# A pooled-mixer layer: a hand-written step order replaced by a planned instruction order, two products accumulated in PSUM, and the last two products done row by row

## The chip, the cores and the metric

One core of one Trainium2 chip runs the whole program. The metric is the device time of one execution in microseconds (us); lower is better. The kernel before was timed three times.

## The reference, cut to what matters

With the given depth of 1 only the pooled mixer runs, and then a layer norm over the sum of the scaled input and the mixer's output. All data is float32; the sequence has 2048 positions, the model width is 1024.

```python
h = x @ w_in                                   # 1024 -> 2 * 2048
u, z = h[..., :D_POOL], h[..., D_POOL:]
...
for g, w in enumerate((2, 4, 8, 16)):          # four groups of 512 channels
    outs.append((c - lag) / cnt - u[:, :, g])  # mean of the last w positions, minus u
m = einsum('bsgc,gcd->bsgd', stack(outs), w_grp).reshape(B, S, D_POOL) * scale
y = (m * silu(z)) @ w_out                      # 2048 -> 1024
out = layer_norm(DN_ALPHA * x + y, ln_g, ln_b)
```

## The kernel before, in words

**Stages.** The group matrix commutes with the pooling over positions, so the kernel first multiplies the u half of `w_in` by `w_grp` (`fold`, 16 steps, four per group) and stores the product in DRAM (`wv_d`). Then it takes the sequence in two halves `h` of 1024 positions. For each half it makes, for eight column pairs `p` in the order 4, 5, 6, 7, 2, 3, 0, 1, one block of z and one block of the values v (`up`, kinds z and v, 256 columns each), pools v along positions, gates it with silu(z) and the scale, and stores the result in DRAM (`g_d`). Then `down` multiplies the stored blocks by `w_out`, adds the scaled input and does the layer norm. So the stages are: fold, ups of half 0, down of half 0, ups of half 1, down of half 1.

**Arithmetic.** Every product is done to nearly float32 accuracy: each operand is split into a high part (a copy to the 32-bit replicated format on ScalarE, line 116) and a low remainder (a subtraction on VectorE, line 117), and one product is three matmuls: high times high, high times low, low times high (`mm3`, lines 122 to 124). A block product of 2 by 2 blocks is done with seven block products and not eight (Strassen-Winograd). The sums of blocks that this needs are VectorE work: of the left and right operands before (lines 129 to 134, 280 to 290, 582 to 588), and of the results after. `fold` has 8 `mm3` in a step; one `up` has 7 products of 4; one `down` has 7 products over 8 values of `k` and 4 row blocks `m`. All matmuls are 128 by 128 by 512.

**Results in `up`.** Seven products go to three PSUM banks Y, Z, W. The first product is copied from Y to SBUF, the second (Z) is added there, and further products are accumulated onto Y and W in PSUM; ScalarE copies from the banks (line 328) and VectorE adds (line 331). Where a combination is missing it is made by adding two SBUF blocks (line 331 with `dest(0, 1)` as operand). A z block passes through silu (lines 328 and 355). A v block is then pooled by repeated shifted additions (line 373), scaled and reduced by v (line 383), gated (line 391), and its block sums are made; three DMAs store it (lines 414 to 416). At the end of a `down`, `read` adds bank and residual into row tiles (lines 492, 494) and takes statistics (496); `norm` (503 to 512) makes the layer norm of a block of 128 rows, with a power on GpSimd for the reciprocal root (505), and stores it (515, 517).

**What sets the order.** The work is a list of `steps`, each of which is the matmuls of one step and the reads of their banks. Loads and splits are `Job`s with `Part`s, taken strictly in one written order. Pooling, sums and norms are `Task`s in a queue with a written due step. After the matmuls of each step, the loop at the end of the file spends a budget (`BUDGET`, in arbitrary units) on the next parts and the most urgent tasks. A load is issued when its place in a ring is free: `raw` tiles hold loaded operands (three places of 8 KB per partition, shared by loads of the fold, x, z, v, `w_out` and the residual), `w2` tiles hold split operands (five places), z tiles two, the v tile one, and the n tiles for the pooling two. Every DMA goes through SyncE's queue (SPq). What is written here is a program order; the framework beneath it assigns semaphores and may itself move an instruction on a queue.

**Last product.** In the down of half 1 the last of the seven products runs row by row: all its operands are split beforehand into tiles freed by x (`spare`), and each of the four row blocks is finished, read and normalised before the next.

Of the kernel before, what the change touches and what calls it, by code (L numbers as in the profile page):

```python
# [12 lines left out]
P = 128  # L13
# [3 lines left out]
NG = 4  # L17
# [10 lines left out]
MT = HS // P  # L28
B = 512
OFF = 16  # L30
# [3 lines left out]

W2 = 5
RAW = 3
BUDGET = 4.2
# [7 lines left out]
A_SLOT = (0, 1, 4, 3, 5, 6, 2)  # L45


class Task:


    def __init__(self, ready, due, cost, run):
        self.ready, self.due, self.cost, self.run = ready, due, cost, run
# [3 lines left out]
def pool_mixer_kernel(ctx: ExitStack, tc, x, xT, wuT, wz, wg, scale, wo, ln_g, ln_b, out):  # L56
# [9 lines left out]
    nc = tc.nc  # L66

# [18 lines left out]
    wv_d = [dr.tile([P, 2, KD // 2, 2 * P], F32, name=f"wv{p}") for p in range(NP)]  # L86
    g_d = [[dr.tile([P, 7, B], F32, name=f"g{h}_{p}") for p in range(NP)] for h in range(2)]
    wt_d = [dr.tile([P, 4, B], F32, name=f"wt{k}") for k in range(NP)]

# [3 lines left out]
    def psum():  # L93
        return ps.tile([P, B], F32, name="acc")

    stores = []
    taken = {"raw": 0, "w2": 0}
    places = {"raw": RAW, "w2": W2}

    def take(kind):  # L100

        for t in [t for t in stores if t[2] is not None and t[2][0] == kind and t[2][1] <= taken[kind] - places[kind]]:
            stores.remove(t)
            t[1]()
        taken[kind] += 1

    def raw_tile():
        take("raw")
        return rp.tile([P, 4, B], F32, name="raw")

    def w2_tile():
        take("w2")
        return wp.tile([P, 2, 2, B], F32R, name="w2")

    def split(hi, lo, src):
        nc.scalar.activation(hi, src, AF.Copy)  # L116
        nc.vector.tensor_sub(lo, src, f32(hi))  # L117

    def mm3(o, a, b, first, last):

        (ah, al), (bh, bl) = a, b
        nc.tensor.matmul(o, ah, bh, start=first, stop=False, skip_group_check=True)  # L122
        nc.tensor.matmul(o, ah, bl, start=False, stop=False, skip_group_check=True)  # L123
        nc.tensor.matmul(o, al, bh, start=False, stop=last, skip_group_check=True)  # L124

    def sums(t, a11, a21, a12, a22):

        def one():
            nc.vector.scalar_tensor_tensor(t[:, 0], a21, -1.0, a22, op0=OP.mult, op1=OP.subtract)
            nc.vector.scalar_tensor_tensor(t[:, 1], t[:, 0], -1.0, a11, op0=OP.mult, op1=OP.subtract)  # L130

        def two():
            nc.vector.tensor_sub(t[:, 2], a11, a21)
            nc.vector.tensor_sub(t[:, 3], a12, t[:, 1])
        return one, two


    steps = []
    jobs = []
    queue = []  # L140
    now = [-1]
    written = set()

    def step(run, reads=()):
        steps.append((run, list(reads)))
        return len(steps) - 1

    class Part:


        def __init__(self, first, last, cost, run, w2=True, ready=-1):
            self.first, self.last, self.cost, self.run, self.w2, self.ready = first, last, cost, run, w2, ready

    class Job:


        def __init__(self, raws, load, parts, until=None, needs=()):
            self.raws, self.load, self.parts, self.until, self.needs = raws, load, parts, until, needs
            self.left, self.loaded = len(parts), False

        def done(self):
            return self.left == 0 and (self.until is None or now[0] >= self.until)

    def store(f, late=2, place=None):

        stores.append((now[0] + late, f, place))

    def later(ready, due, cost, run):
        queue.append(Task(ready, due, cost, run))


    accs = {}

    def fold(g, c):
        me, w = {}, {}

        def load():
            r = g * GC + c * P
            me["raw"] = raw = raw_tile()
            nc.sync.dma_start(raw[:, 2], wg[g, c * P:(c + 1) * P, :])  # L180
            for b in range(2):
                nc.sync.dma_start(raw[:, b], wuT[r:r + P, b * B:(b + 1) * B])

        def part0():
            w["g"] = t = w2_tile()
            split(t[:, 0, 0], t[:, 1, 0], me["raw"][:, 2])

        def part1():
            w["u"] = t = w2_tile()
            for b in range(2):  # L190
                split(t[:, 0, b], t[:, 1, b], me["raw"][:, b])

        def run():
            if c == 0:
                accs[g] = [psum() for _ in range(KD)]
            for m in range(KD):
                cols = slice((m % 4) * P, (m % 4 + 1) * P)
                mm3(accs[g][m], (w["u"][:, 0, m // 4, cols], w["u"][:, 1, m // 4, cols]),
                    (w["g"][:, 0, 0], w["g"][:, 1, 0]), c == 0, c == KC - 1)

        def evict():
            for half in range(2):
                e = zp.tile([P, 4, B], F32, name="z")
                for k in range(4):
                    if k % 2 == 0:
                        nc.scalar.activation(e[:, k], accs[g][half * 4 + k], AF.Copy)  # L206
                    else:
                        nc.vector.tensor_copy(e[:, k], accs[g][half * 4 + k])

                def out_(half=half, e=e):  # L210
                    for q in range(2):
                        nc.sync.dma_start(wv_d[2 * g + q][:, half], e[:, :, q * 2 * P:(q + 1) * 2 * P])
                        written.add(("wv", 2 * g + q, half))
                store(out_, 1)

        s = step(run, [evict] if c == KC - 1 else [])
        jobs.append(Job(1, load, [Part(s, s, 1, part0), Part(s, s, 2, part1)]))


    xh, xl = {}, {}  # L220

    def x_job(h, k, half, first, ready):
        me = {}
        Q = B // 2
        cols = slice(half * Q, (half + 1) * Q)

        def load():
            me["raw"] = raw_tile().rearrange("p a (b c) -> p (a b) c", b=2)
            for a in range(2):
                kk = k + a * KD // 2  # L230
                src = xT[kk * P:(kk + 1) * P, h * HS:(h + 1) * HS].rearrange("p (a b) -> p a b", a=2)
                nc.sync.dma_start(me["raw"][:, 2 * a:2 * a + 2], src[:, :, cols])

        def p0():
            if half == 0:
                xh[h, k] = xp.tile([P, 7, B], F32R, name="xh")
                xl[h, k] = xp.tile([P, 7, B], F32R, name="xl")
            raw = me["raw"]
            me["sums"] = sums(raw[:, 4:8], raw[:, 0], raw[:, 1], raw[:, 2], raw[:, 3])
            me["sums"][0]()  # L240

        def p1():
            me["sums"][1]()

        def part(a, b, c):
            return lambda: split(xh[h, k][:, a:a + c, cols], xl[h, k][:, a:a + c, cols], me["raw"][:, b:b + c])

# [4 lines left out]
    zs = {}  # L252

    def up(h, p, kind):
        me, w, acc = {}, {}, {}
        base = len(steps)


# [478 lines left out]
```

## Time and profile before

| | |
|---|---|
| median of 3 runs | 1066.22 us (1066.04 to 1067.38) |
| the profiled execution: time, span | 1066.48 us, 1064.7 us |
| matmuls | 4435, of them 19 to warm up |
| busy: PE, VectorE, ScalarE, GpSimd | 1023.5, 825.0, 418.6, 30.6 us |
| moved by DMA | 186.39 MB, 175 GB/s on the mean |

The span is the time from the first to the last instruction of the trace. In the trace PE is TensorE's matmuls, PEld its weight loads, DVE VectorE, ACT ScalarE, POOL GpSimd, SPq SyncE's queue of DMA issues. Line numbers are those of the kernel above. A row of the windows view gives, for a stretch of time, each engine's busy time and, in brackets, how many instructions began in it, then the clock that TensorE was granted, the share of the DMA engines' time that was used, and the rate. In a row of the timeline, "[3.12 <-ACT z L328]" says that the engine stood idle for 3.12 us before it and what released it. A busy matmul row is longer than the distance to the next one, because matmuls are pipelined.

### The profile page before, as it was taken

To read this page: it belongs to the slowest core of one execution; us is meant where nothing else is said; L and a number is where in the kernel's file an instruction comes from. 1 tells how busy PE (TensorE), PEld (TensorE's weight loads), DVE (VectorE), ACT (ScalarE), POOL (GpSimd) and SP (SyncE) were. 2 spreads that over 40 slices of the span, in tenths; PEclk is the share of its full clock that TensorE was granted. 3 is DMA by queue.
4 is the path that set the end of the run, shared out by engine and by line. 5 is a ranking of instruction groups with operands and counts; after the bars stand their busy time and mean duration, and the time that the engine had idled before them with its cause. 6 is when DMAs were issued, how large, how long until landed. Compare 5 with 4: busy or idle time off the path is not lost.

```text
span 1064.7 us, 11976 instructions
## 1 busy us (share of the span) xinstructions
PE 1023.5 (96%) x4435; PEld 833.7 (78%) x4435; DVE 825.0 (77%) x1057; ACT 418.6 (39%) x546; POOL 30.6 (3%) x45
## 2 busy tenths in 40 slices
PE   9899899999989999899999999999999999999994
PEld 7777788787868888787788787888878888888883
DVE  6777586988868975887689996968868876765678
ACT  5564433343333334254453343433333334343430
POOL 0000000000000000000002200000000000000003
PEclk9999999999999999899999999999999999999998
DMA  8887525344343355686777423312222325777743
GB/s 263 251 271 253 188 74 193 141 166 148 128 178 148 133 191 192 213 270 223 232 237 257 158 90 99 114 74 109 89 100 109 135 82 190 260 251 238 233 163 158
DMA packets 78746, 186.39 MB, mean 175 GB/s; under 512 B 7392, under 2 KB 24288, under 8 KB 71520
## 3 DMA queue, kind: packets, MB, share of 16 engines
q1 hardware_dynamic: 78688, 185.64, 50.3%
q8 instruction: 34, 0.56, 0.2%
q14 instruction: 24, 0.20, 0.1%
HBM read 131.08 MB, written 54.53 MB: 174 GB/s over the span
## 4 chain that ended last, share of the span: by engine, by line
PE 54%; DVE 23%; DMA 13%; issue 5%; ACT 3%; SPq 1%; POOL 0%; DVEq 0%; POOLq 0%; ACTq 0%
PE acc L122 18%; PE acc L124 18%; PE acc L123 18%; DVE w L117 6%; DMA raw<-in_xT 3%; DMA raw<-wt 3%; DVE n L373 3%; DMA g<-v 2%; DVE xl L117 2%; DVE z L391 1%; DVE n L383 1%; ACT w L116 1%; DMA raw<-in_wo 1%; DVE stats L496 1%; DVE z L512 1%
## 5 line engine op out<-in xcount | busy, mean ns | idle before, releaser
L117 DVE TENSOR_TENSOR w<-raw,w 128x1024 fp32r<-128x1024 f32 (+1 forms) x280 | 295.4, 1067 | 130.7 <-ACT w L116 128.6
L116 ACT ACTIVATE w<-raw 128x1024 fp32r<-128x1024 f32 (+1 forms) x280 | 258.5, 935 | 332.3 <-PE acc L124 131.5
L122 PE MATMUL acc<-xh,w 128*128 128x512 f32 x896 | 350.6, 394 | 11.2 <-ACT z L328 7.1
L124 PE MATMUL acc<-xh,w 128*128 128x512 f32 x896 | 348.2, 391 | 1.8 <-DVE w L117 1.8
L123 PE MATMUL acc<-xl,w 128*128 128x512 f32 x896 | 349.7, 390 | 0.0
L122 PEld LDWEIGHTS acc<-xh,w 128*128 128x128 f32 x896 | 168.9, 189 | 54.4 <-ACT z L328 9.6
L124 PEld LDWEIGHTS acc<-xh,w 128*128 128x128 f32 x896 | 168.7, 188 | 39.4 <-DVE w L117 3.7
L123 PEld LDWEIGHTS acc<-xl,w 128*128 128x128 f32 x896 | 169.1, 189 | 34.1
L122 PE MATMUL acc<-w 128*128 128x512 f32 x416 | 163.2, 396 | 6.1 <-ACT w L116 6.1
L123 PE MATMUL acc<-w 128*128 128x512 f32 x416 | 164.5, 395 | 1.5 <-DVE w L117 1.5
L124 PE MATMUL acc<-w 128*128 128x512 f32 x416 | 163.9, 394 | 0.0
L122 PEld LDWEIGHTS acc<-w 128*128 128x128 f32 x416 | 79.4, 191 | 24.1 <-ACT w L116 7.4
L123 PEld LDWEIGHTS acc<-w 128*128 128x128 f32 x416 | 79.6, 191 | 19.3 <-DVE w L117 2.5
L328 ACT ACTIVATE v<-acc 128x512 f32<-128x512 f32 x80 | 46.3, 597 | 118.8 <-PE acc L124 108.4
L124 PEld LDWEIGHTS acc<-w 128*128 128x128 f32 x416 | 79.5, 191 | 16.6
L328 ACT ACTIVATE z<-acc 128x512 f32<-128x512 f32 x80 | 47.3, 595 | 85.0 <-PE acc L124 69.8
L116 ACT ACTIVATE xh<-raw 128x1024 fp32r<-128x1024 f32 (+2 forms) x52 | 38.0, 730 | 53.3 <-DMA raw<-in_xT 31.6
L373 DVE TENSOR_TENSOR n<-n 128x1024 f32<-128x1024 f32 (+3 forms) x48 | 58.5, 1220 | 0.2
L122 PE MATMUL acc<-w,w 128*128 128x512 f32 x128 | 50.2, 392 | 3.6 <-ACT z L206 3.1
L124 PE MATMUL acc<-w,w 128*128 128x512 f32 x128 | 50.0, 392 | 1.7 <-DVE w L117 1.6
L123 PE MATMUL acc<-w,w 128*128 128x512 f32 x128 | 49.9, 390 | 0.0
L373 DVE TENSOR_TENSOR n<-v 128x1030 f32<-128x1030 f32 (+3 forms) x32 | 39.2, 1229 | 12.5 <-ACT v L328 12.5
(79 smaller groups left out, 695.8 us busy)
## 6 DMA issues: line engine op xcount, KB each, us to landing
raw<-g SPq DMA_DIRECT2D x112, 256.0 KB, 4.2
raw<-in_wz SPq DMA_DIRECT2D x16, 1024.0 KB, 4.8
raw<-wv SPq DMA_DIRECT2D x16, 1024.0 KB, 5.2
g<-v SPq DMA_DIRECT2D x16, 1024.0 KB, 5.0
raw<-wt SPq DMA_DIRECT2D x64, 256.0 KB, 4.5
raw<-in_wo SPq DMA_DIRECT2D x48, 256.0 KB, 4.7
raw<-in_wuT SPq DMA_DIRECT2D x32, 256.0 KB, 5.4
raw<-in_xT SPq DMA_DIRECT2D x32, 256.0 KB, 5.1
```

The lines of the kernel that those rows point to most:

```text
L116: nc.scalar.activation(hi, src, AF.Copy)
L117: nc.vector.tensor_sub(lo, src, f32(hi))
L122: nc.tensor.matmul(o, ah, bh, start=first, stop=False, skip_group_check=True)
L123: nc.tensor.matmul(o, ah, bl, start=False, stop=False, skip_group_check=True)
L124: nc.tensor.matmul(o, al, bh, start=False, stop=last, skip_group_check=True)
L328: return lambda: nc.scalar.activation(o(), a(), func)
L373: nc.vector.tensor_add(n[:, lo:], s[:, lo:], s[:, lo - d:OFF + HS - d])
L383: nc.vector.scalar_tensor_tensor(s[:, OFF:], s[:, OFF:], 1.0 / win, v[:, OFF:], op0=OP.mult, op1=OP.subtract)
L391: nc.vector.scalar_tensor_tensor(z, state[c][:, OFF:], sc[:, t:t + 1], z, op0=OP.mult, op1=OP.mult)
L496: nc.vector.bn_stats(stats[h, half, m][:, n, :], r)
L512: nc.vector.scalar_tensor_tensor(r[:, cols], r[:, cols], rstd, shift[:, cols], op0=OP.mult, op1=OP.add)
```

## The change

Four things change; the arithmetic of the layer and the 1472 `mm3` stay.

**The order.** `steps`, `Job`, `Part`, `Task` and the budget loop go. Every instruction (an `mm3` counts as one) is now an `Op` with an engine, a modelled cost, and the cells of the tiles that it reads and writes; `Plan.add` turns these into dependences, and `Ring` adds those of the tile places. `Plan.record` first gives each `Op` a due time, backwards from the matmuls laid end to end at 0.68 us for an `mm3`; then it simulates five queues and a DMA bus and takes, wherever an engine is free, the ready `Op` with the earliest due time. The instructions are issued in the order that this gives. The order of the matmuls among themselves is the written one.

**PSUM.** In `up` the products run 1, 5, 6, 2, 7, 3, 4 on banks Y, V, X. ScalarE copies product 1 from Y to X, and products 6, 7 and 4 accumulate onto X; 3 accumulates onto product 5 in V, 2 onto product 1 in Y. The two additions of SBUF blocks per pair and the separate silu of a 512-column z block go.

**The last two products by rows.** In the down of half 1, products 3 and 4 run row by row, alternating, and after each the rows are read and normalised. Operands of both are split into the tiles freed by x and into the `w2` ring. Residuals are loaded into the row tiles themselves, and the products of both downs run in the order 1, 2, 6, 5, 7, 3, 4.

**Tiles and transfers.** `raw` becomes six places of 4 KB per partition; x's loads and sums use the n ring and no longer `raw`. z and v weights come in two loads of 512 KB in place of one of 1024 KB, stored block sums of `w_out` and of g in smaller pieces as well. A bank of the fold is copied by whichever of ScalarE and VectorE the plan finds free. For the window of 2 the shifted addition and the mean become one subtraction, with half of the scale. ScalarE's silu table is loaded at the start by a dummy activation.

```diff
-RAW = 3
-BUDGET = 4.2
+RAW = 6
...
+DVE_FIX, DVE_COL = 0.155, 1.04e-3
+ACT_FIX, ACT_COL = 0.21, 0.84e-3
+MM3 = 0.68
+ISSUE = 0.42
+RATE = 0.33
+LANDING = 2.0
+AHEAD = 3.0
+SEEN = {"PE": 0.35, "ACT": 0.15, "DVE": 0.15, "POOL": 0.25}
+WAIT = 0.15
...
+    def record(self):
+        t = 12.0
+        for o in self.ops:
...
+            if o.eng == "PE":
+                o.due = t
+                t += o.cost
...
+        for o in reversed(self.ops):
+            late = min((s.due for s in o.then), default=t + 10 + 1e-3 * o.n)
...
+            gone = LANDING + o.size / RATE / 1e3 if o.size else SEEN[o.eng if isinstance(o.eng, str) else "DVE"]
+            late -= o.cost + gone
+            o.due = min(o.due, late) if o.eng == "PE" else late
...
+                first = min(max(free[e], est[o], bus - AHEAD if o.size else 0.0) for o in can)
+                o = min((o for o in can if est[o] <= first + WAIT), key=lambda o: (o.due, o.n))
...
+        product(1, "Y", 0, 0, True)
+        act(B, lambda: nc.scalar.activation(acc["X"].tile, acc["Y"].tile, AF.Copy), [acc["Y"]["d"]], [acc["X"]["d"]])
+        product(5, "V", 1, 0, True)
+        copy(1, 1, "V")
+        product(6, "X", 1, 1, False)
+        copy(1, 0, "X")
+        product(2, "Y", 0, 1, False)
+        copy(0, 0, "Y", fin)
+        product(7, "X", 2, 0, False)
+        add(1, 1, "X")
+        product(3, "V", 3, 0, False)
+        add(1, 0, "V")
+        product(4, "X", 2, 1, False)
+        copy(0, 1, "X", fin)
...
+        load_rows([(0, m) for m in range(4)] + [(1, 0), (1, 1)])
+        n = 0
+        for j in (1, 2, 6, 5, 7) if h == 1 else (1, 2, 6, 5, 7, 3, 4):
...
+                if h == 0 and n % 3 == 0 and n // 3 <= 8:
+                    x_job(1, (n // 3 - 1) // 2, (n // 3 - 1) % 2)
...
+        spare = [(xhs if i % 2 == 0 else xls).take() for i in range(8)]
+        ops = {}
+        for i, k in enumerate(ORDER):
+            ops[3, k] = spare_step(3, k, spare[i])
+        for i, k in enumerate(ORDER):
+            ops[4, k] = rest_step(4, k, spare[2 * i:2 * i + 2]) if i < 4 else step_of(4, k)
+        for m in range(4):
+            for j, bank, half in ((3, Z, 0), (4, Y, 1)):
+                for i, k in enumerate(ORDER):
+                    mm(bank, ops[j, k], m, False, i == NP - 1)
+                read(j, m)
+                norm(half, m, 4 if (half, m) == (1, 3) else 1)
```

More of the change, by code (lines that the diff above doesn't have):

```diff
@@ new lines, with __init__, take @@
+class Ring:
+    def __init__(self, plan, n, make):
+        self.plan, self.n, self.make, self.bufs, self.made = plan, n, make, [], 0
+    def take(self, make=None):
+        b = Buf(self, len(self.bufs))
+        b.make = make or self.make
+        b.gate = Op(None, 0, None)
+        b.gate.before = [o.gate for o in self.bufs[-1:]]
+        if b.index >= self.n:
+            b.gate.before += self.bufs[b.index - self.n].users
+        b.gate.n = len(self.plan.ops)
+        self.plan.ops.append(b.gate)
+        self.bufs.append(b)
+        return b
@@ L90, in f32, with cell @@
+    rstds = Ring(plan, 4, lambda: sm.tile([P, 1], F32, name="rstd"))
+    statss = Ring(plan, 8, lambda: sm.tile([P, 2, 6], F32, name="stats", bufs=8))
+    cells = {}
+    def cell(*key):
+        return cells.setdefault(key, Cell())
     def f32(ap):
         return ap.bitcast(F32)
[L93 to L172, printed above, removed]
-    def fold(g, c):
[L175 to L206, printed above, removed]
-                    else:
[L208 to L217, printed above, removed]
@@ L220, in pool_mixer_kernel @@
-    xh, xl = {}, {}
-    def x_job(h, k, half, first, ready):
-        me = {}
-        Q = B // 2
-        cols = slice(half * Q, (half + 1) * Q)
[L227 to L246, printed above, removed]
-        fs = ((1.4, p0), (1.4, p1), (2.4, lambda: (part(0, 0, 1)(), part(1, 2, 2)())), (2, part(3, 4, 4)))
-        return Job(1, load, [Part(first, first, c, f, w2=False, ready=ready) for c, f in fs])
@@ L607, in pool_mixer_kernel @@
                 up(h, p, kind)
[L608 to L610 removed]
+                if h == 0 and (i, kind) in RIGHT:
+                    right_sums(ORDER[RIGHT.index((i, kind))])
         down(h)
[L612 to L622 removed]
@@ L636, in pool_mixer_kernel @@
-    users = [q for j, q in parts if q.w2]
-    need = len(steps)
-    for j, q in reversed(parts):
-        q.need = need = min(need, q.first)
-    at = {"load": 0, "part": 0}
-    def load():
-        while at["load"] < len(jobs):
-            j = jobs[at["load"]]
-            if not written.issuperset(j.needs) or not all(o.done() for o in owners[:max(0, taken["raw"] + j.raws - RAW)]):
-                return
-            if j.load is not None:
-                j.load()
-            j.loaded = True
-            at["load"] += 1
@@ L652, in next_part @@
-    def next_part():
-        if at["part"] == len(parts):
-            return None
-        j, q = parts[at["part"]]
-        old = taken["w2"] - W2
-        if not j.loaded or q.ready > now[0] or (q.w2 and old >= 0 and users[old].last > now[0]):
-            return None
-        return q
-    def run_part():
-        j, q = parts[at["part"]]
-        q.run()
-        j.left -= 1
-        at["part"] += 1
-        load()
-        return q.cost
-    load()
-    while (q := next_part()) and q.need <= 1:
-        run_part()
@@ L699, in pool_mixer_kernel @@
-    for t in stores:
-        t[1]()
-    assert not queue and at["part"] == len(parts) and at["load"] == len(jobs)
+    plan.record()
 _OUT = (1, S, D)
```

805 lines of the change are left out of this document (468 added, 337 removed).

## The prediction

> **What bounds the kernel now.** I cut the span at the borders of the five stages, which I found by counting matmuls (fold 16·8·3 = 384, ups of a half 8·2·28·3 = 1344, down of a half 7·8·4·3 = 672), and asked the windows view for these stretches. The columns are the stretch and its length, the busy time of PE, PEld, DVE, ACT and POOL (with counts), the granted clock, the DMA share and GB/s.
>
> ```profile
> 0.00:5.32 5.32, 3.68 (x19) 2.45 (x19) 0.88 (x4) 2.54 (x3) 0.41 (x6) 1.00 0.62 170
> 5.32:98.87 93.55, 88.76 (x384) 71.61 (x385) 69.96 (x123) 51.09 (x86) 0.00 (x0) 1.00 0.84 271
> 98.87:419.12 320.25, 310.55 (x1345) 252.85 (x1344) 252.26 (x317) 118.44 (x164) 3.06 (x14) 0.99 0.44 159
> 419.12:586.73 167.61, 159.94 (x673) 130.10 (x672) 135.56 (x177) 72.94 (x79) 7.16 (x5) 0.96 0.70 231
> 586.73:898.11 311.38, 308.06 (x1346) 250.78 (x1344) 246.94 (x296) 118.26 (x162) 9.29 (x12) 1.00 0.31 113
> 898.11:1050.43 152.32, 152.32 (x673) 125.94 (x671) 108.11 (x124) 55.34 (x53) 6.42 (x5) 1.00 0.65 219
> 1050.43:1064.70 14.27, 0.16 (x1) 0.00 (x0) 11.32 (x21) 0.00 (x0) 4.21 (x4) 0.67 0.39 147
> ```
>
> The down of half 1 is the yardstick: 672 matmuls in 152.32 us without a gap, 0.22667 us each. At this pace the 4416 matmuls need 1001.0 us. What the other stages take beyond it is stall: fold 93.55 - 87.04 = 6.5, ups of half 0 320.25 - 304.64 = 15.6, down of half 0 167.61 - 152.32 = 15.3, ups of half 1 6.7, down of half 1 none; 44.1 in all. With the 5.3 before the first real matmul and 14.3 behind the last this is the span: 5.3 + 1001.0 + 44.1 + 14.3. So TensorE sets the end, and the only things to be won are 44.1 us of stalls and some of 19.6 us at the ends.
>
> Next, the waits and the long gaps one by one: PE's rows of the timeline for the first wait and the six longest, what ScalarE waited for just before four of them, and two stretches with the clock.
>
> ```profile
> 12.72 0.50 PE L124 MATMUL acc<-w,w 128*128 128x512 f32 x1 [0.96 <-DVE w L117]
> ...
> 53.20 0.50 PE L122 MATMUL acc<-w,w 128*128 128x512 f32 x1 [2.73 <-ACT z L206]
> 110.08 0.79 PE L122 MATMUL acc<-xh,w 128*128 128x512 f32 x1 [3.12 <-ACT z L328]
> 298.10 0.79 PE L122 MATMUL acc<-xh,w 128*128 128x512 f32 x1 [3.58 <-ACT z L328]
> 441.59 0.80 PE L122 MATMUL acc<-w 128*128 128x512 f32 x1 [3.27 <-ACT w L116]
> 487.02 0.49 PE L122 MATMUL acc<-w 128*128 128x512 f32 x1 [1.44 <-ACT w L116]
> 518.62 0.50 PE L122 MATMUL acc<-w 128*128 128x512 f32 x1 [1.43 <-ACT w L116]
> ...
> 109.44 0.60 ACT L328 ACTIVATE z<-acc 128x512 f32<-128x512 f32 x1 [2.12 <-DMA wv<-z]
> 297.45 1.09 ACT L328 ACTIVATE z<-acc 128x512 f32<-128x512 f32 x2 [4.50 <-DVE v L134]
> 440.48 2.00 ACT L116 ACTIVATE w<-raw 128x1024 fp32r<-128x1024 f32 x2 [9.49 <-DMA raw<-g]
> 485.91 2.22 ACT L116 ACTIVATE w<-raw 128x1024 fp32r<-128x1024 f32 x2 [2.99 <-DMA raw<-wt]
> ...
> 110.00:120.00 10.00, 9.91 (x37) 7.91 (x38) 3.20 (x4) 4.58 (x7) 0.00 (x0) 0.84 0.48 172
> 440.00:450.00 10.00, 8.41 (x24) 6.67 (x25) 6.47 (x8) 5.08 (x5) 0.00 (x0) 0.66 0.60 215
> ```
>
> The engines that feed TensorE have time (the ACT column adds to 418.6 us, 39%); each gap is an order fault. At 53.20 and 110.08 banks are emptied late, once behind splits and once behind a store of the fold; at 298.10 ScalarE stood behind pooling and sums on VectorE; at 441.59 the last g block came back late from DRAM; at 487.02 and 518.62 loads came late through three coarse `raw` places. A long gap also costs clock: 24 matmuls began between 440 and 450, where 44 fit.
>
> **The change, part by part.** *Matmuls.* 1472 `mm3` before and after: no term of 1001.0 changes, if 0.22667 us holds.
>
> *Vector and scalar work removed.*
>
> ```profile
> L331 DVE TENSOR_TENSOR v<-v 128x512 f32<-128x512 f32 x16 | 11.0, 689 | 13.7 <-ACT v L328 13.7
> L331 DVE TENSOR_TENSOR z<-z 128x512 f32<-128x512 f32 x16 | 10.9, 682 | 1.1 <-ACT z L328 1.1
> L328 ACT ACTIVATE z<-z 128x512 f32<-128x512 f32 x16 | 10.0, 626 | 4.4 <-DVE z L331 4.3
> L383 DVE SCALAR_TENSOR_TENSOR n<-n,v 128x1024 f32<-128x1024 f32 x32 | 38.8, 1214 | 0.0
> L328 ACT ACTIVATE v<-acc 128x512 f32<-128x512 f32 x80 | 46.3, 597 | 118.8 <-PE acc L124 108.4
> 250.00:300.00 50.00, 45.64 (x196) 36.73 (x195) 42.71 (x53) 17.31 (x24) 0.33 (x2) 0.98 0.41 151
> ...
> g<-z SPq DMA_DIRECT2D x16, 256.0 KB, 2.0
> raw<-g SPq DMA_DIRECT2D x112, 256.0 KB, 4.2
> ```
>
> VectorE loses the 32 additions of SBUF blocks (11.0 + 10.9 us) and, for the window of 2, 8 of the 32 means (8·1.21 = 9.7); ScalarE loses 10.0 us of silu. All of it lies beside matmuls: worth nothing directly, but it is slack where VectorE is 85% busy (250 to 300, the window of 16) and where the 298.10 gap arose.
>
> *The copy from bank to bank.* Five reads of banks per `up` by ScalarE before, five after; one now writes PSUM. No row has that form. The nearest is the copy from a bank to v, 597 ns. I bound it by the pace of queued copies below and this row above (0.5 to 0.6 us) and take 0.6. Product 5 covers it: 12 matmuls, 2.72 us. Before, four reads on ScalarE had one product as their cover; now two have, and one addition on VectorE (7 onto X, before 4). If the cover were gone, 32 copies would cost 19 us; I count 0. The reordered copies of the fold, bounded by 0.59 and 0.68 us for a bank on either engine, likewise lie beside matmuls.
>
> *The stalls.* Fold: the plan reads a bank as soon as it is due and loads x behind the fold's own operands, so 53.20 (about 3) and the 1.0 us at 12.72 should go, with a quarter us of restart each; 2.3 are left. The same bytes must pass in less time, which I charge with 0.7: 3.0. Ups of half 0: 110.08 and 298.10 cost about 5 each with their slow clock; 5.4 are left of 15.6, waits of about 1 us for splits, of which I keep half: 2.5. Down of half 0: the g chain can now be added up. From the end of the last product: copy 1.0, window-2 subtraction and gate 2.4 (1.2 each, as the L383 row), store of 256 KB 2.0, load 4.2 (rows above), split on both engines 2.2: 11.8 us against 7 steps of 2.72 = 19.0 before TensorE needs it. The first piece no longer waits for the sums, and the 6.4 us around 441.59 go. Of the 8.7 around 487.02 and 518.62 I keep 3.5, since this stage has most to do: 135.6 us of VectorE work in what would be 152.3. Ups of half 1: 1.5 of 6.7. Down of half 1: 0. The sum is 10.5; with no fault left it is 0, with a third of every stall left 15.
>
> *The end.* VectorE, the last rows, and the DMA issues behind them:
>
> ```profile
> 1054.55 0.64 DVE L492 SCALAR_TENSOR_TENSOR n<-raw,acc 128x512 f32<-128x512 f32 x1
> 1055.16 1.27 DVE L510 SCALAR_TENSOR_TENSOR n<-n,mv,gain 128x1024 f32<-128x1024 f32 x1
> 1056.36 0.69 DVE L496 BATCH_NORM_STATS2 stats<-n 128x6 f32<-128x512 f32 x1
> 1056.96 1.27 DVE L512 SCALAR_TENSOR_TENSOR n<-n,rstd,shift 128x1024 f32<-128x1024 f32 x1
> 1060.96 0.88 DVE L512 SCALAR_TENSOR_TENSOR n<-n,rstd,shift 128x256 f32<-128x256 f32 x2
> 1059.88 2.39 SPq L515 DMA_DIRECT2D out_y<-n x4
> ```
>
> The last matmul begins at 1050.2, but its bank is read only at 1054.55: VectorE is behind. A row block costs it 0.60 + 0.60 + 0.18 + 2·1.20 = 3.8 us (starts of successive rows), and the norms of both halves, 8 blocks or 30 us, fall into the 21.8 us of the last product. With two products by rows they have 43.5 us. The tail is then its own chain: 0.9 to read the bank, and from the statistics at 1056.36 to the end at 1064.70 8.3 us less the foreign row of 1.2 at 1056.96: 8.1 (0.9 + 7.2; about 7.3 at the least, 14.3 if the backlog stays). By rows, all 16 operand sets must be there about 119 us into the stage: 29.4 MB and 4.2 of residuals less 3.1 loaded ahead, 256 GB/s against 219 now; the stage has no gap to lose beforehand, and I count 0.
>
> *DMA.* The loads cut in two add about 64 issues to SPq, of 0.6 us at most (2.39 for four, above): 38 of its 1065 us. In the fold 12.6 MB of weights, 4.2 of x, 6.3 of stores and 1.0 of z weights must pass by about 90 us, 274 GB/s and more.
>
> ```profile
> 80.00:90.00 10.00, 9.39 (x41) 7.36 (x41) 7.50 (x15) 4.88 (x8) 0.00 (x0) 1.00 1.04 336
> raw<-in_wz SPq DMA_DIRECT2D x16, 1024.0 KB, 4.8
> ```
>
> With transfers of 256 and 512 KB the engines were full at 336 GB/s, so there is room of a sixth; a quarter of 1024 KB lands in 4.2 us against 4.8, so cutting adds latency but is hidden by loading ahead. The Trainium skill speaks against cutting transfers: "DMA: Bandwidth & Descriptors", section Bandwidth, says to batch to 1 MiB or more for three quarters of the peak, with 341 GB/s measured at 1 MB and 138 at 64 KB. This trace shows the rate of 1 MB with smaller ones queued behind each other, so the measurement decides; if 256 to 512 KB ran at an estimated 240 GB/s between those two figures of the page, the fold would take 100 us and the sum would be some 10 us more.
>
> **The sum.** 5.3 + 1001.0 + 10.5 + 8.1 = 1024.9 us of span. The profiled execution took 1066.48 for a span of 1064.7 and lies 0.26 above the median, so 1.5 is added: **1026.5 us**.
>
> **The rivals.** *A, transfers.* The order is good, but fold and down of half 0 are fed no faster. For it: the fold used 84% of the DMA time already, and x's loads for half 1, now in the n ring ahead of two residual blocks, must pass within 24 of the down's 56 steps: about 27 MB in the first 87 us, 275 GB/s even with 3 MB loaded ahead. Against it: those late residuals may lag by a product before a bank is needed. Both stages keep their stalls, 6.5 and 15.3: 1024.9 + 3.5 + 11.8 + 1.5 = 1041.7.
>
> *B, the plan is not what runs.* TensorE's rows show that a queue isn't in the order written even now:
>
> ```profile
> 407.40 0.39 PE L124 MATMUL acc<-xh,w 128*128 128x512 f32 x1
> 407.63 0.39 PE L122 MATMUL acc<-w 128*128 128x512 f32 x1
> 410.50 0.50 PE L122 MATMUL acc<-xh,w 128*128 128x512 f32 x1 [0.22 <-ACT v L328]
> ```
>
> From 407.63 eleven matmuls without an x operand, of the down, run ahead of the rest of the last `up`. If whatever moves them undoes the plan too, the 44.1 stay and the tail alone is won: 1066.2 - 6.2 = 1060.0. Against it: a plan that issues nothing before its modelled time leaves little reason to move.
>
> *C, slower: SPq blocked by its stores.*
>
> ```profile
> SPq L414 <- DVE z L391: 171.2, 15, 19.6
> ```
>
> A store of g at the head of SPq waits 11.4 us on the mean, 19.6 at most, for the gate. Now four stores per pair stand in one fixed order with the next loads. A z load held behind one has as cover one `up`, 84 matmuls or 19.0 us, less 4.8 to land (the row of in_wz) and 2.2 for the split: 12.0. Every us beyond is lost in each of 16 pairs. From 14.4 us held (2.5·16 = 40) the kernel is slower than before; at 16 it takes 1026.5 + 16·4.1 = 1092. Against it: the plan models this queue too, and loads far ahead of need are due first.
>
> **How the numbers follow.** Forecast 0.57 (its own range 1018 to 1037: stalls of 2 to 21 us), A 0.24, B 0.11, C 0.08. The range 1016 to 1048 holds the forecast and A; below 1016 there is nothing, as 5.3 + 1001.0 + 7.3 + 1.5 = 1015. Under 0.2% a measurement can't tell a change. C gives slower 0.08; of B 0.03 ends as no change; faster gets 0.89.
>
> **What would show it.** Right: by stage, at most 3 to 4 us beyond the count times 0.22667; a clock of 1.00 in all five; VectorE's read of the last bank within 1 us of the last matmul and about 8 us behind it; VectorE some 30 us less busy. A shows as gaps ended by loads in fold and down of half 0 with DMA shares above 0.85, B as gaps spread as before and matmuls of later stages in between, C as PE waits on z splits whose loads were issued right behind a store. A pace other than 0.22667 in a stage without waits, or waits of product 6 for the bank copy, would make the forecast wrong at its base.

## The result and the profile after

The changed kernel takes 1017.57 us (median of 4, 1017.36 to 1017.85) against 1066.47 us for the kernel before in the same comparison. The ratio is 0.9541, with an interval of 0.9524 to 0.9557. The forecast was 1026.5; the time lies at the lower end of the range of 1016 to 1048.

The windows view of the changed kernel, cut again at the stage borders found by counting matmuls (columns as before):

```profile
0.00:4.94 4.94, 3.89 (x19) 2.77 (x20) 1.04 (x5) 2.75 (x4) 0.35 (x5) 1.00 0.57 182
4.94:92.27 87.33, 87.33 (x386) 72.35 (x385) 64.16 (x95) 54.18 (x78) 0.00 (x0) 1.00 0.84 296
92.27:397.28 305.01, 305.01 (x1345) 252.09 (x1344) 238.91 (x296) 112.55 (x155) 3.17 (x15) 1.00 0.48 170
397.28:549.60 152.32, 152.32 (x673) 126.13 (x672) 129.96 (x173) 73.41 (x81) 3.31 (x3) 1.00 0.76 252
549.60:854.36 304.76, 304.76 (x1346) 252.14 (x1344) 235.56 (x279) 110.94 (x151) 10.26 (x14) 1.00 0.33 116
854.36:1007.37 153.01, 152.62 (x673) 125.87 (x671) 114.02 (x134) 55.64 (x57) 10.46 (x7) 1.00 0.64 217
1007.37:1015.70 8.33, 0.15 (x1) 0.00 (x0) 4.91 (x12) 0.00 (x0) 0.66 (x1) 0.79 0.33 126
```

The pace is the same: 672 matmuls in 152.32 us, now in the down of half 0. Each stage lasts as long as its matmuls: 87.33 for 87.04, 305.01 and 304.76 for 304.64, 152.32 and 153.01 for 152.32. The stalls have gone from 44.1 us to 1.5. The other terms are 4.9 us in front and 8.3 behind: 4.9 + 1001.0 + 1.5 + 8.3 = 1015.7, the span. The clock is 1.00 in every stage ahead of the tail. The waits view, which leaves out the shortest waits, names two waits of TensorE in the whole execution, and the first is the warm-up:

```profile
PE acc L735 <- DVE mhalf L702: 1.1, 1, 1.1
PE acc L306 <- DVE w L299: 0.4, 1, 0.4
```

The rest of the 1.5 us is made of single matmuls that start up to 0.3 us late. The shares by engine of the chain that ended last, from its page, say the same:

```profile
PE 97%; DMA 1%; DVE 1%; issue 0%; ACT 0%; DVEq 0%; SPq 0%; ACTq 0%
```

In the tail VectorE has caught up. Its rows of the timeline behind the last matmul, which begins at 1007.14:

```profile
1007.56 0.69 DVE L635 SCALAR_TENSOR_TENSOR n<-n,acc 128x512 f32<-128x512 f32 x1 [0.67 <-PE acc L307]
1008.28 0.69 DVE L641 BATCH_NORM_STATS2 stats<-n 128x6 f32<-128x512 f32 x1
...
1009.33 1.67 DVE L657 SCALAR_TENSOR_TENSOR n<-n,mv,gain 128x256 f32<-128x256 f32 x4
1010.91 1.67 DVE L660 SCALAR_TENSOR_TENSOR n<-n,rstd,shift 128x256 f32<-128x256 f32 x4
```

VectorE waited 0.67 us for the last bank; before, the bank waited 4 us for VectorE.

### The profile page after: what moved, and what is told of

Same layout as the page of the kernel before. It is cut to its first block, busy times and chain, and to the rows that moved or that the text cites. A ratio compares the mean times of both kernels' runs of the same rounds, so it can differ in the third digit from the quotient of the medians.

```text
span 1015.7 us, 12020 instructions
## 1 busy us (share of the span) xinstructions
PE 1006.1 (99%) x4435; PEld 831.3 (82%) x4435; DVE 788.6 (78%) x989; ACT 409.5 (40%) x524; POOL 28.2 (3%) x45
## 2 busy tenths in 40 slices
DMA packets 80794, 186.39 MB, mean 184 GB/s; under 512 B 8416, under 2 KB 17120, under 8 KB 80736
## 4 chain that ended last, share of the span: by engine, by line
PE 97%; DMA 1%; DVE 1%; issue 0%; ACT 0%; DVEq 0%; SPq 0%; ACTq 0%
PE acc L305 32%; PE acc L306 32%; PE acc L307 32%; DMA n<-in_x 1%; DMA z<-in_x 1%; PE acc L735 0%; DVE w L299 0%; DVE n L657 0%; DVE z L528 0%; DVE n L505 0%; DVE n L660 0%; ACT w L298 0%; DVE stats L641 0%; DVE n L635 0%; DVEq L769 0%
## 5 line engine op out<-in xcount | busy, mean ns | idle before, releaser
L299 DVE TENSOR_TENSOR w<-raw,w 128x1024 fp32r<-128x1024 f32 (+1 forms) x254 | 289.5, 1144 | 125.0 <-ACT w L298 117.5
L298 ACT ACTIVATE w<-raw 128x1024 fp32r<-128x1024 f32 (+1 forms) x254 | 251.1, 997 | 282.4 <-PE acc L307 147.0
L306 PE MATMUL acc<-w 128*128 128x512 f32 x400 | 155.7, 389 | 0.4 <-DVE w L299 0.4
L307 PE MATMUL acc<-w 128*128 128x512 f32 x400 | 155.6, 389 | 0.0
L305 PE MATMUL acc<-w 128*128 128x512 f32 x400 | 155.6, 389 | 0.0
L306 PEld LDWEIGHTS acc<-w 128*128 128x128 f32 x400 | 75.1, 188 | 16.3 <-DVE w L299 0.8
L307 PEld LDWEIGHTS acc<-w 128*128 128x128 f32 x400 | 75.1, 188 | 15.7
L305 PEld LDWEIGHTS acc<-w 128*128 128x128 f32 x400 | 75.1, 188 | 15.5
L468 ACT ACTIVATE z<-acc 128x512 f32<-128x512 f32 x64 | 38.2, 597 | 99.7 <-PE acc L307 99.6
L468 ACT ACTIVATE v<-acc 128x512 f32<-128x512 f32 x64 | 37.2, 595 | 75.4 <-PE acc L307 61.8
L298 ACT ACTIVATE xh<-n 128x256 fp32r<-128x256 f32 (+2 forms) x48 | 33.8, 706 | 46.2 <-DMA n<-in_xT 32.1
L471 DVE TENSOR_TENSOR v<-v,acc 128x512 f32<-128x512 f32 x32 | 22.0, 687 | 35.1 <-PE acc L307 35.0
```

The lines of the kernel that those rows point to most:

```text
L298: act(cols, lambda: nc.scalar.activation(hi(), src(), AF.Copy), R, H)
L299: dve(cols, lambda: nc.vector.tensor_sub(lo(), src(), f32(hi())), [*R, *H], L)
L305: nc.tensor.matmul(acc, ah, bh, start=first, stop=False, skip_group_check=True)
L306: nc.tensor.matmul(acc, ah, bl, start=False, stop=False, skip_group_check=True)
L307: nc.tensor.matmul(acc, al, bh, start=False, stop=last, skip_group_check=True)
L468: act(B, lambda: nc.scalar.activation(dest(c, half), acc[b].tile, func), [acc[b]["d"]], [me[c, half]])
```

## The experiments

Each was timed against runs of the kernel before on its own chip, whose medians were 1064.5 to 1066.5. For each I also measured from its trace what every stage lasted beyond its matmuls' count times 0.22667 us. All figures are in us; "front" is the time before the first real matmul, "tail" that behind the last one's slot. "Time" is the median, while the stages are those of the one profiled execution; this took 2.4 us less than the median in e2 and 3.0 less in e4, and lies within 1.2 of it elsewhere. A difference of about 3 us or less between two runs is not settled by the intervals of their ratios.

```
kernel                       front  fold  ups0  down0  ups1  down1  tail   time   ratio to before
before                         5.3   6.5  15.6   15.3   6.7    0.0  14.3  1066.5
changed                        4.9   0.3   0.4    0.0   0.1    0.7   8.3  1017.6  0.9541 (0.9524-0.9557)
e1 order, rings, small parts   5.3   1.0   3.7    0.0   1.9    0.8  10.4  1025.6  0.9619 (0.9583-0.9654)
e2 written order in the plan   4.9   2.0   3.2   10.0   3.9    1.1   8.2  1038.5  0.9739 (0.9704-0.9774)
e3 flat costs                  4.9   0.3   3.5    4.5   0.5    0.0   8.3  1025.8  0.9621 (0.9589-0.9653)
e4 before, two products rows   5.2   4.5  15.7   14.3   6.3    1.5   8.2  1061.6  0.9953 (0.9936-0.9970)
e5 old products                5.3   0.6   4.7    0.0   1.9    0.7   8.3  1024.1  0.9610 (0.9583-0.9637)
e6 one product by rows         4.9   0.7   0.7    0.0   0.2    0.8  10.5  1020.6  0.9576 (0.9549-0.9603)
e7 before, new products        5.1   7.2   6.1    8.9   5.5    0.0  14.6  1050.7  0.9862 (0.9831-0.9894)
e8 copy without cover          4.8   0.8   7.0    0.0   4.6    0.3   8.3  1029.2  0.9666 (0.9631-0.9701)
e9 e7 and VectorE work         5.2   6.4   8.7   12.0   4.3    0.0  14.8  1054.9  0.9896 (0.9857-0.9934)
e10 changed and VectorE work   5.2   0.7   0.9    0.4   0.4    0.2   8.3  1019.1  0.9560 (0.9531-0.9589)
e11 loads cut again            5.2   0.3   0.8    0.0   0.3    0.8   8.4  1018.7  0.9558 (0.9529-0.9586)
e12 four raw places            5.1   3.2   3.6    0.0   0.0    7.1   9.0  1031.1  0.9668 (0.9633-0.9703)
```

**The order and the rings alone.** The changed kernel with the old products of e5, the single product by rows of e6 (both edits are shown below), and

```diff
-RIGHT = ((0, "v"), (1, "v"), (4, "z"), (4, "v"), (5, "z"), (5, "v"), (6, "z"), (6, "v"))
+RIGHT = tuple((i, "v") for i in range(8))
...
-    nc.scalar.activation(tiny, tiny, AF.Silu)
```

> The changed kernel with all but the planned order and the new rings undone: the products of an up in the old order on the old banks with the two additions of SBUF blocks and the separate silu of half a z block, one product by rows at the end, the block sums of w_out right behind each v, no silu table load at the start. Theory (order and rings took the stalls, the rows took the tail): 1017.6 + 6 for the tail + at most 1.5 = 1022 to 1027 us, stalls of TensorE under 4 us. Rival (the work taken off VectorE and ScalarE took the stalls of the ups): the 22 us of stalls in both ups come back in good part, 1035 to 1046.

It took 1025.6 us, inside the theory's range, but with 7.4 us of stalls and not under 4. The rows of its windows view for the two ups and for the tail:

```profile
93.32:401.62 308.30, 307.04 (x1346) 251.29 (x1344) 250.43 (x314) 121.15 (x167) 3.25 (x15) 1.00 0.48 169
...
553.94:860.47 306.53, 306.16 (x1346) 251.49 (x1344) 244.24 (x295) 116.76 (x159) 11.38 (x14) 1.00 0.32 115
...
1013.64:1024.10 10.46, 0.16 (x1) 0.00 (x0) 7.30 (x16) 0.00 (x0) 1.20 (x2) 0.62 0.49 192
```

The new order with its rings takes 40.8 of the 48.9 us without the new products and the second product by rows. This run also keeps the small parts of the change (the smaller transfers, the single subtraction for the window of 2, the fold's copies on either engine), so the order is not quite alone. The ups hold 5.6 us of stalls, 5.1 more than in the changed kernel: not the rival's 22, but more than the 1.5 that I had allowed; the tail costs 2.2 and not 6.

**What makes the order.** First the key by which a queue chooses among the ready operations, then the costs:

```diff
-                o = min((o for o in can if est[o] <= first + WAIT), key=lambda o: (o.due, o.n))
+                o = min((o for o in can if est[o] <= first + WAIT), key=lambda o: o.n)
```

> The changed kernel, but of the ready operations each queue takes the one written first, and not the one due earliest; graph, rings and modelled costs stay. Theory (earliest due first is what took the stalls): older work such as pooling and norms goes ahead of splits that TensorE needs sooner, 1035 to 1075 us. Rival (dependence graph and finer rings suffice, whatever the key): within 3 us of 1017.6.

```diff
-DVE_FIX, DVE_COL = 0.155, 1.04e-3
-ACT_FIX, ACT_COL = 0.21, 0.84e-3
+DVE_FIX, DVE_COL = 0.68, 0.0
+ACT_FIX, ACT_COL = 0.68, 0.0
...
-RATE = 0.33
-LANDING = 2.0
+RATE = 1000.0
+LANDING = 0.0
...
-SEEN = {"PE": 0.35, "ACT": 0.15, "DVE": 0.15, "POOL": 0.25}
+SEEN = {"PE": 0.0, "ACT": 0.0, "DVE": 0.0, "POOL": 0.0}
```

> The changed kernel with a blind cost model: every VectorE and ScalarE operation counts 0.68 us, a DMA only its issue, landings and handovers nothing. Theory (the order by due times matters, their accuracy less, but loads are now thought to land at once): the stalls come back in part, 5 to 25 us, 1023 to 1043. Rival (the measured costs in the plan are essential): above 1050. Second rival (costs are irrelevant): within 2 us of 1017.6.

With the written order as the key it took 1038.5, about 21 us more; with blind costs 1025.8, 8 more than the changed kernel. Both lie in the theory's ranges. What the key does is best seen in the down of half 0 of e2: its windows row, TensorE's longest wait in the timeline, and VectorE's timeline in the last 5 us before that.

```profile
401.79:564.14 162.35, 155.33 (x674) 126.91 (x672) 130.84 (x176) 72.63 (x79) 7.28 (x5) 0.98 0.71 237
```

```profile
459.12 0.80 PE L306 MATMUL acc<-w 128*128 128x512 f32 x1 [6.49 <-DVE w L299]
```

```profile
454.39 1.28 DVE L641 BATCH_NORM_STATS2 stats<-z 128x6 f32<-128x512 f32 x2
455.58 0.41 DVE L312 SCALAR_TENSOR_TENSOR n<-n 128x256 f32<-128x256 f32 x1
455.91 0.42 DVE L316 TENSOR_TENSOR n<-n 128x256 f32<-128x256 f32 x1
456.24 0.42 DVE L314 SCALAR_TENSOR_TENSOR n<-n 128x256 f32<-128x256 f32 x1
...
457.85 1.22 DVE L299 TENSOR_TENSOR w<-raw,w 128x1024 fp32r<-128x1024 f32 x1
```

TensorE stands still for 6.5 us while VectorE reads banks, takes statistics and makes the block sums of x for the next half, which only the ups of the next half need, from 564 on; only at 457.85 comes the split that the matmul waits for. VectorE is as busy in this stage as in the changed kernel (130.8 and 130.0 us): it isn't a lack of time but the order. So the graph, the rings, the new products and the rows leave 20.2 us of stalls, and the due time as the key takes all but 1.5 of them. About 8 of the 21 us hang on the modelled costs: with the key kept and every cost blind they are lost again. Engine costs, transfers and handovers were made blind together, so this doesn't say which of them counts.

**The rows at the end.** In the kernel before, the seventh and sixth product of the last down by rows, with operands in the x tiles and `w2`:

```diff
-            by_rows = h == 1 and j == 6
+            by_rows = h == 1 and j >= 5
...
                 for m in range(4):
-                    def run_row(m=m, mm=mm):
...
+                    for jj, b, half in ((5, Z, 0), (6, Y, 1)):
+                        def run_row(m=m, jj=jj, b=b):
...
```

> The kernel before with one part alone: the last two products of the down of half 1 by rows, alternating, operands in the tiles freed by x and in the w2 ring. Theory (the tail was VectorE's backlog of eight norms): read of the last bank within 1 us, 14.3 us behind the last matmul become 8.3, 1060.5 us (1058 to 1063), other stages as before. Rival (sixteen operand sets at once starve TensorE without the plan): a stall of 6 us or more in that stage that eats the gain, 1066 or more.

It took 1061.6 us, ratio 0.9953. The windows rows for the last stage and the tail (the first is cut one matmul, 0.2 us, early at both ends), and then VectorE's read of the last bank from the timeline:

```profile
894.45:1048.32 153.87, 153.20 (x673) 125.81 (x672) 116.56 (x137) 55.84 (x57) 10.19 (x7) 1.00 0.66 224
1048.55:1056.80 8.25, 0.16 (x1) 0.00 (x0) 5.00 (x12) 0.00 (x0) 0.65 (x1) 0.78 0.35 127
```

```profile
1048.74 0.69 DVE L503 SCALAR_TENSOR_TENSOR n<-raw,acc 128x512 f32<-128x512 f32 x1 [0.67 <-PE acc L124]
```

The tail falls from 14.3 to 8.2 as worked out; 1.5 us go into stalls of the stage itself. The opposite edit, one product by rows in the changed kernel:

```diff
-        for j in (1, 2, 6, 5, 7) if h == 1 else (1, 2, 6, 5, 7, 3, 4):
+        for j in (1, 2, 6, 5, 7, 3) if h == 1 else (1, 2, 6, 5, 7, 3, 4):
...
+        ops = [spare_step(4, k, spare[i]) for i, k in enumerate(ORDER)]
...
```

> The changed kernel with only the last product by rows. Theory: 30 us of norms and reads meet 21.8 us of matmuls, VectorE is 6 to 8 us behind at the end, 1023 to 1026 us, all of it behind the last matmul. Rival (the plan itself would have mended the tail by putting the norms of the other half earlier): 1018 to 1020.

1020.6: 3 us more by time and by span, 2.2 of them in the tail. The time alone doesn't settle so small a difference, since the intervals overlap; the tail does. VectorE's rows behind the last matmul, which begins at 1008.03:

```profile
1008.46 0.69 DVE L635 SCALAR_TENSOR_TENSOR n<-n,acc 128x512 f32<-128x512 f32 x1
1009.07 1.28 DVE L657 SCALAR_TENSOR_TENSOR n<-n,mv,gain 128x1024 f32<-128x1024 f32 x1
...
1010.86 1.27 DVE L660 SCALAR_TENSOR_TENSOR n<-n,rstd,shift 128x1024 f32<-128x1024 f32 x1
```

The run lies between my two cases and nearer the rival: under the plan VectorE reads the last bank at once, and of its backlog only two rows of another block's norm, 1.3 us each, are left in the tail.

**The products.** The old order of the products, its banks and its additions in the changed kernel:

```diff
-        act(B, lambda: nc.scalar.activation(acc["X"].tile, acc["Y"].tile, AF.Copy), [acc["Y"]["d"]], [acc["X"]["d"]])
-        product(5, "V", 1, 0, True)
-        copy(1, 1, "V")
-        product(6, "X", 1, 1, False)
-        copy(1, 0, "X")
-        product(2, "Y", 0, 1, False)
-        copy(0, 0, "Y", fin)
-        product(7, "X", 2, 0, False)
-        add(1, 1, "X")
...
+        copy(0, 0, "Y")
+        product(2, "X", 0, 1, True)
+        add(0, 0, "X")
+        product(6, "Y", 1, 1, False)
+        copy(1, 0, "Y")
+        if kind == "z":
+            act(B, lambda: nc.scalar.activation(dest(0, 0), dest(0, 0), fin), [me[0, 0]], [me[0, 0]])
+        product(5, "V", 1, 0, True)
+        copy(1, 1, "V")
+        product(7, "Y", 2, 0, False)
+        copy(0, 1, "Y")
+        dve(B, lambda: nc.vector.tensor_add(dest(1, 1), dest(1, 1), dest(0, 1)), [me[0, 1], me[1, 1]], [me[1, 1]])
...
```

> The changed kernel with the products of an up in the old order on banks Y, Z, W: no copy between banks, 32 additions of SBUF blocks and 16 silus of 512 columns back. Theory (that work is only slack under the new order): VectorE 22 us and ScalarE 10 us busier, 1017.6 to 1019.5 us. Rival (the slack is what keeps TensorE fed, above all with the window of 16): 1025 or more, stalls where VectorE is busiest.

1024.1 us, 6.5 more, and the interval of its ratio lies clear above that of the changed kernel: between theory and rival, nearer the rival. TensorE's waits now name the reads of banks by ScalarE (L468):

```profile
PE acc L305 <- ACT v L468: 1.3, 3, 0.5
PE acc L305 <- ACT w L298: 1.3, 2, 0.8
...
PE acc L305 <- ACT z L468: 0.5, 1, 0.5
```

What stood in the way of one of them is seen in the rows of ScalarE and TensorE:

```profile
320.77 0.64 ACT L481 ACTIVATE z<-z 128x512 f32<-128x512 f32 x1 [1.43 <-DVE z L471]
321.31 1.06 ACT L468 ACTIVATE v<-acc 128x512 f32<-128x512 f32 x2
321.94 0.50 PE L305 MATMUL acc<-xh,w 128*128 128x512 f32 x1 [0.46 <-ACT v L468]
```

The silu of half a z block (L481), which this edit brings back, stands at the head of ScalarE's queue until VectorE's addition is done, and the copy of the bank that TensorE needs comes behind it.

The same part alone in the kernel before (the sequence of banks, products and reads as in the changed one, no more):

```diff
-        banks = "YZYWYWY"
+        banks = "YVXYXVX"
...
+        def across():
+            acc["X"] = psum()
+            nc.scalar.activation(acc["X"], acc["Y"], AF.Copy)
...
```

> The kernel before with one part alone: the new order of the products of an up, the copy of product 1 from bank to bank and the accumulation onto it. Theory (saved VectorE and ScalarE work is worth nothing without the order): 1064 to 1068 us, VectorE 22 us less busy. Rival (the slack itself closes gaps): 1056 to 1062, the gap near 298 us gone.

It missed both ranges on the far side: 1050.7 us, ratio 0.9862. The stalls of the first ups fall from 15.6 to 6.1, those of the first down from 15.3 to 8.9 (both rows are cut one matmul, 0.2 us, early):

```profile
99.31:409.83 310.52, 307.06 (x1344) 251.06 (x1343) 243.98 (x304) 114.92 (x158) 4.66 (x14) 1.00 0.45 164
409.83:571.05 161.22, 156.33 (x673) 126.64 (x672) 133.31 (x176) 71.81 (x78) 7.16 (x5) 0.99 0.73 240
```

Is that VectorE's time, or that fewer products must wait for a read with only one product between? Two runs put the time back, with 32 additions whose results nobody uses (the line of the first):

```diff
+            lambda: nc.vector.tensor_add(spoil, dest(1, 1), dest(1, 1))],
```

> The kernel before with the new products alone, as in the run that took 1050.7, and 32 additions of 512 columns put back on VectorE, whose results nobody uses. It parts the two things that the new products bring: VectorE time, and fewer bank reads with only one product as cover. Theory after that run (the covers are what counts, the time of VectorE hardly): 1049 to 1054 us. Rival (22 us of VectorE time are what counts): 1060 to 1066.

> The changed kernel with the same 32 useless additions on VectorE, in the plan. Theory (covers): the 6.5 us that the old products cost under the plan were bank reads without cover, so 1017.5 to 1019. Rival (VectorE time): 1022 to 1024.5, as with the old products.

In the kernel before it took 1054.9 (span 1052.5 for 1048.4), 0.9 above the theory's range; the intervals of the ratios overlap, so the 4 us aren't settled, but by the medians they aren't the whole gain of 13.8 (1064.5 to 1050.7, in its own comparison). In the changed kernel it took 1019.1, which can't be told from 1017.6. So by the medians VectorE's time is worth some 4 us under the old order and 1.5 under the new one, neither of them settled. What is left of the effect of the products, some 10 and some 5 us, goes with something that these two runs did not put back: the closely covered reads, or the 16 silus that the new products take off ScalarE. The rows at 320.77 show that such a silu can hold a bank's copy back. Which of the two counts, and for how much, was argued and not shown by a run of its own.

**The cover of the copy.** Product 6 ahead of product 5:

```diff
+        product(6, "X", 1, 1, False)
+        copy(1, 0, "X")
         product(5, "V", 1, 0, True)
         copy(1, 1, "V")
-        product(6, "X", 1, 1, False)
-        copy(1, 0, "X")
```

> The changed kernel with product 6 written ahead of product 5, so that the bank that product 6 accumulates onto is copied with no product between. It measures what the cover of the copy is worth. Theory (matmuls run in the order written): 32 times a copy of 0.6 us and two handovers of 0.2 to 0.4, 1.0 to 1.4 us each: 1050 to 1062 us. Rival (whatever moves matmuls on TensorE's queue puts product 5 back in between): within 3 us of 1017.6, with product 5 ahead in the trace.

1029.2 us: neither 1050 nor 1018. The ups hold 11.6 us of stalls, 11.1 more than in the changed kernel. One of the 32 blocks in TensorE's and ScalarE's rows of the timeline:

```profile
135.15 0.39 PE L305 MATMUL acc<-xh,w 128*128 128x512 f32 x1
135.38 0.39 PE L306 MATMUL acc<-xl,w 128*128 128x512 f32 x1
135.60 0.39 PE L307 MATMUL acc<-xh,w 128*128 128x512 f32 x1
135.98 0.50 PE L305 MATMUL acc<-xh,w 128*128 128x512 f32 x1
136.32 0.39 PE L306 MATMUL acc<-xl,w 128*128 128x512 f32 x1
```

```profile
135.35 0.58 ACT L475 ACTIVATE acc<-acc 128x512 f32<-128x512 f32 x1 [1.60 <-PE acc L307]
```

The copy runs from 135.35 to 135.93, and TensorE starts product 6 at 135.98, 0.15 us later than the pace would have it; the matmul behind it is 0.11 late as well. Thirty of the 32 blocks look like this one, to the hundredth, and lose 0.26 us each; the first block loses 1.4 and another 0.6, and a wait for a read by VectorE costs 0.8. But three matmuls come between product 1 and product 6. They can't be of product 1, whose end released the copy, nor add onto the banks that the copy reads and writes; so they are the first `mm3` of product 5, which was written behind product 6 and runs ahead of it. So something beneath the written order does move matmuls, by a small number, and here it hides 0.68 us in a block.

**Transfers.** Loads of z and v weights cut once more, four of 256 KB for an up, and then four raw places in place of six:

```diff
+                def halves(c=c, b=b):
+                    for i in range(2):
+                        nc.sync.dma_start(b.tile[:, i], wz[p, c][:, i * B:(i + 1) * B])
+                dma(512, halves, [], [b["d"]])
...
```

> The changed kernel with every load of z and v weights cut once more, four of 256 KB for two of 512 KB. Theory (transfers queue behind each other at a full rate, and loads run far ahead): 1017 to 1018.5. Rival (transfers under 1 MiB cost bandwidth, which is short in the fold and where a pair starts): 1020 to 1026, with gaps ended by loads at the start of the ups.

```diff
-RAW = 6
+RAW = 4
```

> The changed kernel with four raw places for six; an up takes all four at a time. Theory (loading ahead is what emptied the downs of stalls, 8.7 us of them in the kernel before): the loads of the next up or step are issued only when a place is split and free, 10 to 60 us of stalls in the ups and some in the downs, 1027 to 1080. Rival (the order alone did it): within 3 us of 1017.6.

Cutting the loads changes nothing that can be measured (1018.7, 0.2 above the theory's range; 2 or 3 us would not be seen). Fewer places cost 13.5 us, inside the theory's range, but not where I expected it: the down of half 0 and the second ups have no stall at all, and 7.1 us fall into the stage with the rows, 3.6 into the first ups and 3.2 into the fold. Two rows of the windows view, and one wait of TensorE from the timeline:

```profile
403.44:555.76 152.32, 152.32 (x674) 126.17 (x673) 129.65 (x173) 72.94 (x81) 6.24 (x3) 1.00 0.75 250
...
860.39:1019.77 159.38, 155.78 (x673) 127.59 (x671) 114.23 (x134) 55.80 (x57) 10.45 (x7) 0.98 0.64 213
```

```profile
979.71 0.50 PE L305 MATMUL acc<-xl,xh 128*128 128x512 f32 x1 [2.69 <-ACT xl L298]
```

The first row says that six places are not what emptied the down of half 0; with the due times four are enough there. The wait at 979.71 is for an operand of the second row product: the sixteen sets that are needed within a few us of each other are where the two missing places cost most.

## Why the prediction was right, and where it wasn't

**What bounds.** Right. 0.22667 us per matmul holds to the last digit in a kernel that hardly pauses, and the gain came from the stalls and the tail alone: 42.6 us of stalls, 6.0 of tail, 0.4 in front.

**The stalls, 10.5 us, were the mis-sized term: 1.5 measured.** The failing step is the share that I kept of each stage (3.0, 2.5, 3.5, 1.5, 0), each for a load on an engine or on the transfers that I took to be heavy. The runs show that these loads don't bind. The down of half 0, for which I kept 3.5 because of VectorE's 89%, has 130 us of VectorE work in 152.3 and no stall; with the written order as key the same work gives 10.0. The fold moved 296 GB/s at a DMA share of 0.84 with 0.3 us of stall. A busy share below one told nothing of stalls here; the order within the share did.

**The vector work "worth nothing directly"** was right as to VectorE's time, as far as the intervals go: 36.4 us less of it, and 32 additions put back cost 1.5 us, which can't be told from none. What ScalarE's 10 us are worth was not tried alone. **The copy "I count 0"** was right with its cover, at 582 ns for the 0.6 taken; the price without cover, 19 us, was too high at 11.6 because I didn't reckon with an `mm3` being moved, which hides 0.68 us in a block. The step that failed here stands next to it: I counted the closely covered reads, four by ScalarE before, two by ScalarE and one by VectorE now, and gave the difference no price, nor ScalarE's queue. The old products cost 6.5 us under the plan, and in the old order the new ones won 13.8 by the medians; what in them does it is open. It didn't show in the total, because the parts overlap: order and rings 41, products alone 14, rows alone 5 make 60 for a change of 49.

**The g chain.** The long wait near the start of the down of half 0 is gone, and that down has no stall, but with far less to spare than the sum said. The last product of the ups ends at about 397.4, and TensorE needs the split block at 397.28 + 19.0 = 416.3. The last gate, the issue of its store, and the split on both engines, from the timeline:

```profile
402.61 1.27 DVE L528 SCALAR_TENSOR_TENSOR z<-n,sc,z 128x1024 f32<-128x1024 f32 x1
403.91 0.32 SPq L540 DMA_DIRECT2D g<-z  x1
412.27 1.06 ACT L298 ACTIVATE w<-raw 128x1024 fp32r<-128x1024 f32 x1 [4.11 <-DMA raw<-g]
413.61 1.22 DVE L299 TENSOR_TENSOR w<-raw,w 128x1024 fp32r<-128x1024 f32 x1
```

The chain ends at 414.8, after 17.4 us and not 11.8, with 1.5 us left and not 7. The gate is done 6.5 us behind the product where the sum had 3.4, and from the store's issue to the start of the split 8.4 us pass where it had 6.2. That the conclusion held all the same was in part luck.

**The tail**: 8.1 worked out, 8.3 measured, and 8.2 with the rows alone in the old kernel; the backlog of VectorE was its cause.

**The rivals.** A, transfers, did not happen: the fold and the down of half 0, which it left at 6.5 and 15.3 us of stalls, have 0.3 and none. The Trainium skill's rule to batch transfers to 1 MiB or more ("DMA: Bandwidth & Descriptors", section Bandwidth) spoke for A; halving the loads of z and v again moved nothing that can be measured. These loads serve the ups, where the DMA share is 0.48 and 0.33, so no run here halves transfers where the engines are full. The nearest is the prediction's row at 80.00: 336 GB/s with transfers of 256 and 512 KB, or 331 GB/s up to 87.60, ahead of the first load of 1024 KB. B is real as a mechanism and small in size: matmuls are moved where the written order would make TensorE wait, in e8 three in a block. C did not happen: SPq still waits for gates behind its stores, but none of these waits reaches TensorE. From the waits view of SPq in the changed kernel:

```profile
SPq L540 <- DVE z L528: 81.8, 16, 13.8
SPq L541 <- DVE z L528: 56.5, 15, 7.9
```

The range held the time, barely, and the forecast's own range, 1018 to 1037, missed it by 0.4. Its lower end was the floor itself, and 5.3 + 1001.0 + 8.1 + 1.5 left only 1.7 us between floor and result: a forecast in the middle of a range that ends at a floor was a choice for stalls that no row of the trace demanded.

**Open.** Why the new products alone also take 6 us from the down of half 0 in the old kernel, which they don't touch, was not tried. Nor was it tried to change the number of closely covered reads alone, or to put ScalarE's 16 silus back alone. The small parts of the change (the single subtraction for the window of 2, x in the n ring, residuals loaded into the row tiles, the fold's copies on either engine) were not taken apart from the order.

## What to carry to other kernels

Where one engine should never pause and the others are 40 to 85% busy, cost the stalls by their order: find for each what stood in the queue ahead of the late instruction and when that was needed. Taking the ready operation that is due earliest, counted back from the bound engine, was worth about 20 us of 1017 here, 8 of which hang on costs in the plan that are near the measured ones. Look at what stands ahead of a bank's read in its engine's queue, above all where only one product lies between the read and the bank's next use; what such reads cost was not shown here by themselves. When several repairs aim at the same stalls, measure them alone and together, since their gains need not add.

## What had not been expected of the hardware

TensorE was granted its full clock, 1.00, in all five stages of an execution in which they hold 1.5 us of stalls in a thousand. ScalarE's copy of 128 by 512 values from bank to bank takes less time than from a bank to SBUF:

```profile
L468 ACT ACTIVATE v<-acc 128x512 f32<-128x512 f32 x64 | 37.2, 595 | 75.4 <-PE acc L307 61.8
...
L475 ACT ACTIVATE acc<-acc 128x512 f32<-128x512 f32 x32 | 18.6, 582 | 40.4 <-PE acc L307 40.4
```

582 against 595 ns; the rows of v are plain copies, as that from bank to bank is. The Trainium skill says that ScalarE writes to PSUM faster than to SBUF ("PSUM — Partial Sum Buffer", section Specifications (TRN2)); the trace agrees, by 2.2%.

In the fold, 0.84 of the DMA engines' time carried 271 GB/s before and 296 now. Packets under 2 KB fell from 24288 to 17120 over the whole execution; that these are the cause was not tried.
